# Running sums of the log gates: f32 products replaced by two fp32r passes over split operands

## The chip, the cores and the metric

The kernel runs on one core of one Trainium2 chip. The metric is the device time of one execution in microseconds. The instruction streams of the engines are fixed when the kernel is built; at run time each engine works its own stream off in order and waits at semaphores.

## The reference

One inference step of a hybrid decoder layer, for a prompt of 1024 rows and for 64 sample rows (8 sequences of 8 tokens) with a paged cache. One input projection feeds two groups of heads: gated linear attention (4 heads, dk 64, dv 128) and latent attention (8 heads). Their outputs go through one output projection, a gated MLP with a short convolution, and a gated per-layer embedding. The change touches the linear attention of the prompt:

```python
z = (ga @ lw['gla_w_a2'] + lw['gla_b_a']).astype(jnp.float32)
log_a = (jax.nn.log_sigmoid(z) / GLA_GATE_NORM).reshape(B, T, GLA_HEADS, GLA_DK)   # GLA_GATE_NORM = 16
...
b = jnp.cumsum(log_a, axis=2)              # running sum inside a chunk of tokens
q_dec = q * jnp.exp(b)
k_inv = k * jnp.exp(-b)
k_end = k * jnp.exp(b_last - b)
A = jnp.where(causal, einsum('bnthd,bnshd->bnhts', q_dec, k_inv), 0.0)
...
S = jnp.exp(bl)[..., None] * S + jnp.einsum('bshd,bshv->bhdv', ke, vv)
```

## The kernel before, in words

**Two streams.** The main loop (lines 1598 to 1614) draws from two generators. `dense()` does the prompt: projections of rows 0 to 511 (`prompt_half(0)`), then of rows 512 to 1023 (`prompt_half(1)`), then the linear attention (`gla_prompt`, between its steps also `gla_sample`), then the softmax attention. `cache_stream()` does the attention of the sample rows over the paged cache, in 64 blocks. A block loads `craw` by an indirect DMA on POOL's queue, transposes it on PE (`ctp`, line 522), multiplies it with the weights in `mv` (`ks`, lines 139 to 141, 8 tiles x 2 halves x 3 products), squares and copies the results on ACT (`csq`, `sn`), reduces them on DVE (`css`), adds the rope scores (`csr`), takes the maximum (`mt`), the exponential (`phl`), and multiplies with the values (`cpv`, line 645). POOL works on `sn`, `chl` and `phl`. The generators are interleaved by weights that each dense step yields and by a table `PACE`.

**Who sets the order.** The kernel is written in a tile framework. Tiles come from pools; a tag in a pool names a ring of a few buffers, and a new tile of that tag gets a buffer when an older one has been read for the last time. A scheduler puts the recorded instructions in order for each engine, by their place in the program and by what is ready in its own model of time; so an instruction may stand ahead of others that were written before it. `tc.keep_in_program_order(...)` takes that freedom from an instruction: it stays behind those that were written ahead of it on its engine.

**The second half of the projections.** `prompt_half(1)` transposes its rows (line 798), then computes the latent columns (`ps_lt`, line 278: 4 row tiles x 8 x 3 products of 432 columns). Their weights are loaded through three staging buffers (line 266) and split into a high and a low part (lines 267 to 271). The high parts and half of the low parts lie in three buffers of the ring "w" of the pool `wp`; the other low parts lie in two tiles `wlt` (line 812) of the ring "xin" of the pool `wk`, which has two buffers. The two buffers have held rows of the prompt before (line 769). All further weights of that half (`ps_pj`, `ps_q`, `ps_gv`) come through the same staging buffers and the ring "w".

**The masks.** `gla_weights()` (line 974) is called between the two halves. It builds two masks on POOL, `mq` (128 x 2 x 128) and `mk` (128 x 448), with entries 1/16, 0 and, in `mk`, -1/16; both have buffers of their own in the pool `cp`. The two memsets (lines 982, 983) are kept in program order.

**The step of a tile.** `pre(t)` in `gla_prompt` (line 1138) loads the gate input, `qk` and `gv` of 128 tokens; `log_gate` (line 1004) computes the log gates `la` with a product (`ps_z`, line 1006), three ACT instructions and one of DVE (`z`, line 1012). The running sums are products of `la` with the masks, in f32: four of 128 columns into `ps_b` (line 1149) and two of 448 columns into `ps_bk` (line 1164). ACT takes the exponentials (`qe`, `kx`), DVE scales `q` into `qb` and `qtb` (lines 1156, 1159), POOL scales `k` inside `kx` (line 1168). `local(t)` and `advance(t)` use these for scores, state and output. There are 8 tiles; tile n+2 is in `pre` while n+1 is in `local` and n in `advance`.

`split(hi, lo, src)` (line 115) is used all over the kernel for fp32r operands: ACT copies `src` to `hi` in fp32r, and DVE (or POOL) subtracts, `lo = src - hi`. A product of two split operands is then three single-pass products (`mm3`, line 138).

## Time and profile before

| | |
|---|---|
| times of three runs | 2251.01, 2253.16, 2255.33 us |
| median | 2253.16 us |
| span of the profiled execution, first to last instruction | 2250.3 us |
| mean granted TensorE clock | 0.980 |
| `ps_b` L1149: instructions recorded, median | 64, 275 ns |
| `ps_bk` L1164: instructions recorded, median | 32, 539 ns |
| DMA | 233.60 MB, mean 104 GB/s |

The profiled execution is given by its span; the runs' times include what lies around the span. PE is TensorE (PEld its weight loads), DVE is VectorE, ACT ScalarE, POOL GpSimd, SP the engine that issues most DMAs. L1149 is line 1149 of the kernel. The duration of a matmul in the trace includes its way through the array, so consecutive ones overlap: what a matmul costs in a row of others is the distance from start to start. A row of a timeline or of the chain gives the start, the length and the instruction; a row of a stretch gives its bounds, its length, the busy time and count of PE, PEld, DVE, ACT and POOL, the granted clock, the share of the DMA engines and GB/s; a row of the list of groups gives line, engine, operation, tiles and shapes, count, busy time, mean ns of one, and the idle time ahead of it with what ended it.

### The profile page before, as it was taken

The page shows a single profiled execution, that of the slowest core. Times are in us where ns is not written, and L with a number is a line of the kernel's source. Part 1 is how long each engine was busy: PE and PEld are TensorE (multiplying, and loading weights), DVE is VectorE, ACT ScalarE, POOL GpSimd, SP SyncE. Part 2 cuts the span into 40 slices and gives each one's busy share as a digit, 9 for nine tenths or more (in the row PEclk, how much of TensorE's full clock was granted, in tenths as well). Part 3 has the DMA queues.
Part 4 walks back from the last instruction along what each step waited for, and adds up shares of the span by engine and source line. Part 5 has one row for each costly group of instructions (what it writes and reads, how often), then busy time and mean ns, then how long its engine had stood idle before and what let it go on. Part 6 is the DMA issues. An engine that isn't in the chain of part 4 may idle for free.

```text
span 2250.3 us, 38434 instructions
## 1 busy us (share of the span) xinstructions
PE 2147.8 (95%) x13459; PEld 1937.9 (86%) x13459; DVE 1681.4 (75%) x2490; ACT 1357.9 (60%) x3692; POOL 1356.9 (60%) x1395
## 2 busy tenths in 40 slices
PE   7999989999999999998999988999999999998999
PEld 6889978878888888887888867999999997786899
DVE  4675776467788888886978888888888877966632
ACT  5666766777778898886777775433333334334521
POOL 5675677577777777676455467656566643589000
PEclk9899999999999999999999998999999999999999
DMA  5343244413242222213322222322222228456321
GB/s 184 115 134 102 84 126 147 139 55 88 83 122 59 60 66 74 66 41 100 122 66 78 63 104 62 113 94 90 94 94 96 93 70 291 154 193 206 112 76 37
DMA packets 204547, 233.60 MB, mean 104 GB/s; under 512 B 42430, under 2 KB 146339, under 8 KB 204355
## 3 DMA queue, kind: packets, MB, share of 16 engines
q1 hardware_dynamic: 190691, 184.21, 26.1%
q0 software_dynamic: 12432, 42.48, 6.2%
q10 hardware_dynamic: 1232, 4.46, 0.5%
q8 instruction: 108, 1.77, 0.3%
q14 instruction: 84, 0.69, 0.1%
HBM read 188.52 MB, written 42.52 MB: 103 GB/s over the span
## 4 chain that ended last, share of the span: by engine, by line
PE 71%; DVE 9%; POOL 6%; DMA 5%; ACT 5%; issue 3%; SPq 0%; POOLq 0%; ACTq 0%; DVEq 0%
PE ps_gu L140 7%; PE ps_gu L141 7%; PE ps_gu L139 7%; PE ks L139 4%; PE ks L141 4%; PE ks L140 4%; PE cpv L645 2%; PE ctp L522 2%; DMA raw<-ffn_w_down 2%; PE ps_lt L278 2%; PE ps_pj L139 2%; DVE css L565 1%; PE ps_pj L140 1%; PE ps_pj L141 1%; PE ps_pg L140 1%
## 5 line engine op out<-in xcount | busy, mean ns | idle before, releaser
L560 ACT ACTIVATE csq<-ks 128x256 f32<-128x256 f32 x1040 | 392.4, 400 | 85.6 <-PE ks L141 76.6
L565 DVE TENSOR_REDUCE css<-csq 128x16 f32<-128x1024 f32 (+1 forms) x264 | 315.7, 1197 | 62.9 <-ACT csq L560 59.8
L116 ACT CAST wh<-st 128x512 fp32r<-128x512 f32 x176 | 108.3, 619 | 183.3 <-PE ps_gu L140 163.8
L139 PE MATMUL ks<-mv1h,cTh 128*128 128x320 f32 (+1 forms) x520 | 169.5, 328 | 8.4 <-ACT sn L562 3.6
L139 PE MATMUL ks<-mv0h,cTh 128*128 128x320 f32 (+1 forms) x520 | 170.8, 330 | 6.9 <-ACT csq L560 3.0
L604 POOL TENSOR_TENSOR chl<-craw,chl 128x1024 fp32r<-128x1024 f32 x64 | 141.2, 2206 | 57.3 <-ACT chl L603 56.7
L140 PE MATMUL ks<-mv1l,cTh 128*128 128x320 f32 (+1 forms) x520 | 153.3, 297 | 0.0
L140 PE MATMUL ks<-mv0l,cTh 128*128 128x320 f32 (+1 forms) x520 | 152.1, 294 | 0.0
L141 PE MATMUL ks<-mv0h,cTl 128*128 128x320 f32 (+1 forms) x520 | 147.8, 297 | 0.9 <-DVE cTl L117 0.8
L630 POOL TENSOR_TENSOR phl<-sn,phl 128x512 fp32r<-128x512 f32 (+1 forms) x64 | 84.8, 1326 | 105.0 <-ACT phl L629 104.6
L141 PE MATMUL ks<-mv1h,cTl 128*128 128x320 f32 (+1 forms) x520 | 147.9, 298 | 0.0
L117 DVE TENSOR_TENSOR wl<-st,wh 128x512 fp32r<-128x512 f32 x132 | 119.0, 903 | 29.0 <-ACT wh L116 29.0
L140 PE MATMUL ps_dn<-o 128*128 128x512 f32 x308 | 125.6, 408 | 12.1 <-DVE o L117 12.0
L117 POOL TENSOR_TENSOR wl<-st,wh 128x512 fp32r<-128x512 f32 x44 | 69.1, 1574 | 104.3 <-ACT wh L116 104.3
L139 PE MATMUL ps_dn<-o 128*128 128x512 f32 x308 | 119.6, 399 | 4.5 <-ACT o L116 4.5
L141 PE MATMUL ps_dn<-o 128*128 128x512 f32 x308 | 123.8, 402 | 0.0
L117 DVE TENSOR_TENSOR cTl<-ctp,cTh 128x512 fp32r<-128x512 f32 (+1 forms) x136 | 90.0, 662 | 37.3 <-ACT cTh L116 36.3
L1317 POOL TENSOR_TENSOR pl<-p,ph 128x512 fp32r<-128x512 f32 (+1 forms) x96 | 97.4, 1019 | 33.0 <-DVE ph L1316 23.2
L562 ACT COPY sn<-ks 128x64 f32<-128x64 f32 x520 | 117.1, 225 | 0.0
L139 PEld LDWEIGHTS ks<-mv1h,cTh 128*128 128x128 f32 x520 | 98.8, 190 | 20.7 <-ACT sn L562 7.4
L139 PEld LDWEIGHTS ks<-mv0h,cTh 128*128 128x128 f32 x520 | 97.9, 188 | 20.8 <-ACT sn L562 7.0
L139 PE MATMUL ps_gu<-xrh,wh 128*128 128x320 f32 x352 | 108.6, 309 | 0.9 <-ACT xrh L116 0.9
(675 smaller groups left out, 8019.0 us busy)
## 6 DMA issues: line engine op xcount, KB each, us to landing
raw<-ds SPq DMA_DIRECT2D x77, 256.0 KB
raw<-ffn_w_down SPq DMA_DIRECT2D x66, 256.0 KB
stage<-w_in SPq DMA_DIRECT2D x48, 256.0 KB
st<-ffn_w_gate SPq DMA_DIRECT2D x44, 256.0 KB
st<-ffn_w_up SPq DMA_DIRECT2D x44, 256.0 KB
wr<-ffn_w_down SPq DMA_DIRECT2D x44, 256.0 KB
ds<-cv SPq DMA_DIRECT2D x21, 512.0 KB
oraw<-doT SPq DMA_DIRECT2D x16, 256.0 KB
```

The lines of the kernel that those rows point to most:

```text
L116: act.copy(hi, src)
L117: (lo_eng or dve).tensor_tensor(lo, src, hi.bitcast(F32), ALU.subtract)
L139: pe.matmul(ps, ah, bh, start=first, stop=False)
L140: pe.matmul(ps, ah, bl, start=False, stop=False)
L141: return pe.matmul(ps, al, bh, start=False, stop=last)
L278: pe.matmul(ps, x, w, start=first, stop=last)
L560: act.activation(sq[:, f * 256:f * 256 + 256], ks[:, 0:256], AF.Square)
L562: act.copy(o.sn[:, g0 + i, :], ks[:, 256:320])
L565: dve.tensor_reduce(o.ss[:, g0 + i + 1 - n:g0 + i + 1, :].rearrange("p i h -> p (i h)"), sq2[:, :n].rearrange("p i (h n) -> p (i h) n", n= ...
L604: pool.tensor_tensor(ch[:, c0:c1, 128:256], src, ch[:, c0:c1, 0:128].bitcast(F32), ALU.subtract)
L630: pool.tensor_tensor(phl[:, :nt, 64:128], sb, phl[:, :nt, 0:64].bitcast(F32), ALU.subtract)
L1317: pool.tensor_tensor(pl[:, c0:], p[:, c0:], ph[:, c0:].bitcast(F32), ALU.subtract)
```

## The change

The masks get fp32r buffers of their own (`mqr`, `mkr`). They are built, by the same instructions, in a tile of the ring "xin", and POOL copies them. In the step of a tile the log gates are split in a high and a low half, and each running sum is accumulated over two fp32r products, one for each half. The two parts of `mq` go into one product of 256 columns; for that the axes of `ps_b` and `qe` change places. The reads of `qe` follow.

```diff
@@ -977,8 +977,9 @@
 
         gout = ctile([P, 1], F32, "gout")
         sp.dma_start(gout, A["gla_g_out"].rearrange("o d -> d o"))
-        mq = cst([P, 2, P], F32, "mq")
-        mk = cst([P, 448], F32, "mk")
+        mqr, mkr = cst([P, 2, P], F32R, "mqr"), cst([P, 448], F32R, "mkr")
+        mq = wk.tile([P, D], F32, tag="xin", name="masks")
+        mq, mk = mq[:, 0:256].rearrange("p (i t) -> p i t", i=2), mq[:, 256:704]
         tc.keep_in_program_order(pool.memset(mq, 1.0 / 16))
         tc.keep_in_program_order(pool.memset(mk, 1.0 / 16))
         pool.affine_select(mq, mq, pattern=[[0, 2], [1, P]], compare_op=ALU.is_ge, fill=0.0, base=0, channel_multiplier=-1)
@@ -993,7 +994,9 @@
                                    channel_multiplier=-1)
             if i < 4:
                 pool.tensor_scalar(mk[:, OFFS[i] + 32 * i:OFFS[i + 1]], m4[:, i], -1.0, None, ALU.mult)
-        return gout, mq, mk
+        pool.tensor_copy(mqr, mq)
+        pool.tensor_copy(mkr, mk)
+        return gout, mqr, mkr
 
     def low_rank(g, c0, rows):
 
@@ -1143,30 +1146,36 @@
             gv = g.tile([P, 512], F32, tag="gv", name="gv", bufs=3)
             sp.dma_start(gv, dgv[tt, :])
             la = log_gate(g, gaT, P, wa2)
+            hl = [g.tile([P, 256], F32R, tag="la" + k, name="la" + k) for k in "hl"]
+            split(*hl, la)
+
+            def summed(ps, pr, m):
+                for i, x in enumerate(hl):
+                    pe.matmul(ps, x[:, pr * P:(pr + 1) * P], m, start=i == 0, stop=i == 1)
+
             ps = pd([P, 2, 2, P], "ps_b")
-            for i in range(2):
-                for pr in range(2):
-                    pe.matmul(ps[:, i, pr], la[:, pr * P:(pr + 1) * P], mq[:, i], start=True, stop=True)
+            for pr in range(2):
+                summed(ps[:, pr].rearrange("p i t -> p (i t)"), pr, mq.rearrange("p i t -> p (i t)"))
             qe = g.tile([P, 2, 2, P], F32, tag="qe", name="qe", bufs=3)
             act.activation(qe, ps, AF.Exp)
 
             qbt = qb[t % 2]
             for e in range(2):
                 rr = slice(64 * e, 64 * e + 64)
-                dve.scalar_tensor_tensor(qbt[rr].rearrange("p a i e t -> p (a i) e t")[:, :, e, :],
-                                         qk[rr, 0:2].rearrange("p a (i t) -> p (a i) t", t=32), 0.125,
-                                         qe[rr, 0].rearrange("p a (i t) -> p (a i) t", t=32), ALU.mult, ALU.mult)
-                dve.scalar_tensor_tensor(qtb[t % 3][rr, e::2, :], qk[rr, 0:2], 0.125, qe[rr, 1], ALU.mult, ALU.mult)
+                dve.scalar_tensor_tensor(qbt[rr, :, :, e, :],
+                                         qk[rr, 0:2].rearrange("p a (i t) -> p a i t", t=32), 0.125,
+                                         qe[rr, :, 0].rearrange("p a (i t) -> p a i t", t=32), ALU.mult, ALU.mult)
+                dve.scalar_tensor_tensor(qtb[t % 3][rr, e::2, :], qk[rr, 0:2], 0.125, qe[rr, :, 1], ALU.mult, ALU.mult)
 
             kx = g.tile([P, 2, 448], F32, tag="kx", name="kx")
             for pr in range(2):
                 ps = pd([P, 512], "ps_bk")
-                pe.matmul(ps[:, 0:448], la[:, pr * P:(pr + 1) * P], mk, start=True, stop=True)
+                summed(ps[:, 0:448], pr, mk)
                 act.activation(kx[:, pr], ps[:, 0:448], AF.Exp)
             for i in range(5):
                 w = min(32 * (i + 1), P)
                 pool.tensor_tensor(kx[:, :, offs[i]:offs[i] + w], kx[:, :, offs[i]:offs[i] + w], qk[:, 2:4, 0:w], ALU.mult)
-            dec = [qe[:, 1, pr, P - 1:P] for pr in range(2)]
+            dec = [qe[:, pr, 1, P - 1:P] for pr in range(2)]
             return gv, qbt, kx, dec
 
         def local(t, qbt, kx):
```

## The prediction

> **What bounds the kernel now.** I read the page first, then busy time by stretches, then the chain of waits through the stage that the edit touches.
>
> ```profile
> span 2250.3 us, 38434 instructions
> ...
> PE 2147.8 (95%) x13459; PEld 1937.9 (86%) x13459; DVE 1681.4 (75%) x2490; ACT 1357.9 (60%) x3692; POOL 1356.9 (60%) x1395
> ...
> PEclk9899999999999999999999998999999999999999
> ...
> PE 71%; DVE 9%; POOL 6%; DMA 5%; ACT 5%; issue 3%; SPq 0%; POOLq 0%; ACTq 0%; DVEq 0%
> ```
>
> PE is busy 95% of the span and carries 71% of the chain, so the time is PE's work plus the idle time of PE: 2250.3 = 2147.8 + 102.5. A change counts if it changes either of these. The two stretches below (share of each engine, then granted clock) are the second half of the projections, and the linear-attention stage, which the trace shows from 437.5 us (first ps_z) to 617 us.
>
> ```profile
> 268.00:437.00 169.00, 156.36 (x973) 140.00 (x971) 104.93 (x179) 115.22 (x339) 113.60 (x126) 0.96 0.44 130
> 440.00:620.00 180.00, 175.61 (x1276) 147.73 (x1274) 133.07 (x235) 134.70 (x440) 127.94 (x190) 1.00 0.28 78
> ```
>
> In the linear-attention stage PE has 4.4 us of idle time in 180, DVE and ACT sit at 74 and 75%. All that time the cache stream runs in between: its blocks fill PE wherever the dense stream waits.
>
> **The change part by part. 1: the running sums.** Before, a tile does four f32 products of 128 columns (ps_b) and two of 448 (ps_bk), each recorded as two instructions, so x8 and x4. In the chain (start, length, what) they stand for four of the eight tiles; first and last of the four:
>
> ```profile
> 455.80 0.89 PE ps_b L1149 x8
> 456.69 1.50 PE ps_bk L1164 x4
> ...
> 613.86 0.89 PE ps_b L1149 x8
> 614.75 1.51 PE ps_bk L1164 x4
> ```
>
> That is 2.39 us a tile. After, a tile does four products of 256 columns and four of 448, in fp32r and single pass. Prices of that form: in the timeline three ks products of 256 columns start between 440.68 and 441.03, and the chain has 13 ps_lt products of 432 columns in a row.
>
> ```profile
> 440.68 0.28 PE L139 MATMUL ks<-mv1h,cTh 128*128 128x256 f32 x1
> ...
> 441.03 0.31 PE L139 MATMUL ks<-mv1h,cTh 128*128 128x320 f32 x1
> ...
> 240.58 2.55 PE ps_lt L278 x13
> ```
>
> 256 columns cost 0.35/3 = 0.117 us; 432 cost 2.55/13 = 0.196, so 448 some 0.203. The new tile costs 4 x 0.117 + 4 x 0.203 = 1.28 us, 1.11 less. Over 8 tiles PE loses 8.9 us of work.
>
> **2: the split.** Each tile gains a cast of 128x256 on ACT and a subtraction of 128x256 on DVE, both between z and the first product. Nearest rows:
>
> ```profile
> L116 ACT CAST kTh<-crp 128x256 fp32r<-128x256 f32 x64 | 24.7, 386 | 8.5 <-PE crp L500 7.5 <-DVE css L565 0.3
> L117 DVE TENSOR_TENSOR kTl<-crp,kTh 128x256 fp32r<-128x256 f32 x64 | 26.6, 416 | 20.0 <-ACT kTh L116 19.8
> L117 DVE TENSOR_TENSOR wl<-st,wh 128x512 fp32r<-128x512 f32 x132 | 119.0, 903 | 29.0 <-ACT wh L116 29.0
> ```
>
> ACT 0.39 us. DVE between 0.42 (one operand in PSUM) and 903/2 = 0.45 (both in SBUF, as here): 0.45. So 3.1 us more ACT and 3.6 us more DVE over the stage, both with 45 us of room; what counts is 0.84 us of delay per tile. The products of the low half stand behind cache products in PE's order, so the cache stream covers it where it has work ready. Where the chain runs on ACT or DVE it is paid.
>
> Sum for the stage: the four tiles on the chain gain 1.11 each for certain; of the other four I take half. 6 x 1.11 = 6.7, less the delay for two tiles, 1.7: **-5 us**. Ends: -8.9 (all gained, all delay covered) and -4 x 1.11 + 4 x 0.84 = -1.
>
> The regrouped access of qe and qb leaves counts and elements of the DVE and ACT instructions as they are: nothing. The masks are made by the same POOL instructions and two copies, below.
>
> **3: where the masks are built.** This is the part that the diff hides. mq and mk had a buffer of their own; now they are built in a buffer of the ring "xin" (two buffers), and copied to fp32r. The next users of that ring are the two low halves of the latent weights (wlt, line 812) of the second half of the prompt. The memsets of the masks are kept in program order, so on POOL they come after the work of the cache blocks written ahead of them. Before, that held nobody up: the instruction order on POOL has the first wlt split 46 rows ahead of the memset of mq. In the compiled order of the changed kernel both wlt splits come behind it:
>
> ```
> POOL row 195  L630 phl (cache block)
> POOL row 196  L983 Memset masks
> POOL row 198  L271 wlt (first buffer)
> POOL row 214  L997 mqr<-masks;  row 216  L998 mkr<-masks
> POOL row 219  L271 wlt (second buffer)
> ```
>
> PE follows. Before, the 96 ps_lt products of this half are mixed with 72 cache instructions. After, three ps_lt come early, then none until 192 cache instructions are through (counted from the ks products just ahead of the first ps_lt), then the rest, most of it in one piece. Weights that follow (wp, stage) wait too, because the ps_lt hold their buffers. So for 192 PE instructions, a bit over 2.6 blocks (a block has some 74: 48 ks, 8 cpv, 8 ctp, 2 crp, 6 csr, 2 mt), PE has the cache stream alone. What does that cost? The nearest row is the ten us ahead of the linear-attention stage, where all but two products are the cache's; the best row is five us in which cache and transposes alternate, the worst the second half of the nearest one:
>
> ```profile
> 430.00:440.00 10.00, 7.73 (x56) 7.09 (x57) 5.63 (x7) 7.21 (x26) 10.00 (x15) 1.00 1.11 252
> 230.00:235.00 5.00, 5.00 (x44) 4.99 (x43) 5.00 (x9) 4.87 (x16) 4.66 (x5) 1.00 0.31 91
> 435.00:440.00 5.00, 2.73 (x19) 2.19 (x18) 1.71 (x3) 3.00 (x13) 5.00 (x6) 1.00 1.16 273
> ```
>
> Nearest: 2.27 us idle per 56, so 192/56 x 2.27 = 7.8 us. Best: 0. Worst: 192/19 x 2.27 = 23 us, though POOL is full there with memsets of the next stage. A check by ACT, which must square and copy what PE makes:
>
> ```profile
> L560 ACT ACTIVATE csq<-ks 128x256 f32<-128x256 f32 x1040 | 392.4, 400 | 85.6 <-PE ks L141 76.6 <-DVE css L565 2.9 <-PE csr L141 0.3
> L562 ACT COPY sn<-ks 128x64 f32<-128x64 f32 x520 | 117.1, 225 | 0.0
> L116 ACT CAST cTh<-ctp 128x512 fp32r<-128x512 f32 x128 | 76.0, 594 | 36.2 <-PE ctp L522 35.9
> L603 ACT CAST chl<-craw 128x1024 fp32r<-128x1024 f32 x64 | 67.7, 1057 | 27.9 <-PE cpv L645 11.4 <-issue 8.1 <-POOL sn L594 3.8
> L510 ACT COPY sr<-csr 128x512 f32<-128x512 f32 x64 | 38.7, 604 | 16.5 <-PE csr L141 12.7 <-POOL sn L594 1.6 <-POOL rs_r L112 1.0
> L628 ACT ACTIVATE sn<-sn 128x512 f32<-128x512 f32 x56 | 35.7, 638 | 10.5 <-DVE sn L626 10.5
> L629 ACT CAST phl<-sn 128x512 fp32r<-128x512 f32 x56 | 35.4, 632 | 0.8
> ```
>
> With kTh's 24.7 they make 787.7 us over 64 blocks, 12.3 a block; 2.6 blocks need 32 us of ACT and 192 x 7.73/56 = 26.5 us of PE: 5.5 us idle at least, since ACT would have to run without a gap. I take the nearest row: **+8 us**.
>
> PE's work isn't lost: the cache stream is 112 instructions (1.5 blocks) ahead when the linear attention starts, 108 ahead when the attention starts, level at its end. It comes back as shorter stages. The idle time doesn't: the stages in which it comes back leave PE little idle time (4.4 in 180).
>
> Then the second wlt buffer waits for the mask chain. Before, that chain took, with other POOL work between, from the first to the last of these rows; a copy of 256 columns is the third:
>
> ```profile
> 307.10 0.31 POOL L982 MEMSET mq<- 128x256 f32 x1
> 318.33 1.31 POOL L995 TENSOR_SCALAR mk<-mq 128x32 f32<-128x32 f32 x4
> 293.12 0.46 POOL L944 COPY kt<-lat 128x256 f32<-128x256 f32 x1
> ```
>
> 12.5 us, and 0.46 + 0.80 for the copies: 13.8. PE has, between the first and the second wlt buffer, 54 cache instructions and 18 ps_lt: 54 x 0.138 + 18 x 0.196 = 11.0 us (0.138 is 7.73/56). **+3 us** of waiting, with the ks, csr and cpv of the next block queued behind it on PE; ends 0 (POOL does the chain without a break) and 6 (the cache waits for ACT meanwhile). SP's order loses nothing more: its loads of these weights stand where they stood, and wait for the same buffers.
>
> **Sum:** 2250.3 - 5 + 8 + 3 = 2256.3 us for the profiled execution. The median of the three times shown, 2253.16, lies 2.9 above its span; **2259 us**.
>
> **A rule against the change.** When PE idles the profile shows this, at the hole that the weights' loads leave at 280 us:
>
> ```profile
> 280.00:285.00 5.00, 1.92 (x10) 1.25 (x10) 3.42 (x9) 1.58 (x5) 0.93 (x1) 0.83 0.77 235
> 285.00:290.00 5.00, 3.89 (x11) 3.06 (x12) 2.65 (x4) 3.83 (x12) 2.55 (x2) 0.50 0.68 195
> 350.00:355.00 5.00, 3.02 (x10) 2.80 (x11) 4.95 (x12) 2.68 (x8) 3.53 (x6) 0.65 0.84 233
> 355.00:360.00 5.00, 5.00 (x29) 4.81 (x29) 1.38 (x6) 1.92 (x6) 2.68 (x2) 0.66 1.08 318
> ```
>
> One such hole costs 5 x 0.17 + 5 x 0.50 = 3.4 us of clock beside its idle time, the other 5 x 0.35 + 5 x 0.34 = 3.5. But at 435 us PE was busy 2.73 of 5 at a clock of 1.00: short gaps do not trip it. The Trainium skill, "TensorE: Matmul & The Clock Gate", Part 1: The HAM clock gate, says that an idle window of about 3.4 us halves the clock until a busy window has passed. The trace agrees (0.50 after a hole of 3 us), and by that rule a gap in the cache-only stretch would count only if it is that long.
>
> **The rivals.** A, the forecast, 0.50.
>
> B, the stretch trips the clock: the wait for the masks comes in one piece with nothing of the cache ready. Two holes at 3.5 us on top of the forecast: 2266; or the worst row. For it: PE waits in order, one late ps_lt stops the cache behind it. Against it: the clock of 1.00 at 435 us. 0.14.
>
> C, it comes out even: the cache keeps PE as busy as ACT allows (5.5), the masks are ready in time (0), the stage gains 6: 2253. For it: ACT has 32% of room in the second half. 0.20.
>
> D, faster: the wait takes the place of waits that are there anyway. The trace of before loses 12.6 us of PE between 268 and 437, much of it waiting for weights (the hole at 280 us). If the loads arrive while the cache runs alone, the holes of 275 to 290 us (0.46 + 3.08 + 1.11 = 4.7 and 3.4 of clock) go, and with the 8.9 of the stage against 8 + 3 the time is 2253.2 - 8.9 + 11 - 8.1 = 2247. It decides from the point at which holes of 6 us vanish. Against it: the low halves that wait hold the three staging buffers, so the loads cannot run ahead. 0.16.
>
> That single pass fp32r isn't cheaper I leave out: ks and ps_lt show its price hundreds of times.
>
> **How the numbers follow.** Some 0.2%, 4.5 us, is what a measurement of this kernel can tell from none. A runs from +1 to +12: three quarters of it (0.38) slower, 0.12 within 0.2%. B is slower, C the same, D faster. Slower 0.52, same 0.32, faster 0.16. The range runs from 2246 (D, within a microsecond) to 2272 (stretch near its worst row, or B with a long wait).
>
> **What would show it.** Right: L1154 at some 0.12 and 0.20 us; between 240 and 290 us a stretch with PE at 75 to 85%, ps_lt in two parts around it, and the first ps_z 20 to 30 us later than at 437.5 (112 x 0.138 = 15, and 11 of idle); this lead shrinking to some 6 us by the end of attention. Wrong: PE at 95% or more in that stretch, holes gone at 280 us, or a new hole in the linear-attention stage where PE waits for the split.

## The result, and the profile after

| | median of the runs | runs, lowest to highest |
|---|---|---|
| before | 2252.09 us | 4, 2248.33 to 2255.33 |
| after | 2285.09 us | 4, 2273.94 to 2288.14 |

The ratio is 1.0138, with a 95% interval of 1.0118 to 1.0158. The forecast was 2259, its range 2246 to 2272: the sign was right, the size was not. From the page of the changed kernel, its span, the engines and the shares of the chain:

```profile
span 2284.5 us, 38396 instructions
...
PE 2150.9 (94%) x13427; PEld 1940.8 (85%) x13427; DVE 1691.8 (74%) x2498; ACT 1357.4 (59%) x3700; POOL 1362.4 (60%) x1397
...
PE 50%; DVE 9%; ACT 5%; POOL 4%; issue 3%; DMA 3%; SPq 0%; POOLq 0%; DVEq 0%; ACTq 0%
```

PE's idle time went from 102.5 to 2284.5 - 2150.9 = 133.6 us, and PE's busy time did not fall by the 8.9 us of the forecast, it rose by 3.1. Where this happened is seen when both spans are cut at the same three marks: the first `ps_z`, the first product of the softmax attention, and the first product after it (`pt_cv`). Four stretches of before:

```profile
0.00:437.50 437.50, 402.34 (x2511) 363.87 (x2511) 275.62 (x501) 293.49 (x883) 282.13 (x347) 0.96 0.42 127
437.50:649.40 211.90, 206.93 (x1506) 175.57 (x1507) 158.10 (x276) 158.98 (x523) 149.96 (x212) 1.00 0.30 84
649.40:1144.70 495.30, 476.04 (x3189) 416.24 (x3188) 409.00 (x655) 415.01 (x1237) 345.26 (x346) 0.99 0.27 78
1144.70:2250.30 1105.60, 1062.52 (x6256) 982.19 (x6256) 838.71 (x1060) 490.43 (x1052) 579.53 (x493) 0.98 0.34 110
```

And of after:

```profile
0.00:456.20 456.20, 420.25 (x2625) 379.87 (x2625) 289.16 (x525) 309.90 (x939) 299.81 (x373) 0.98 0.40 124
456.20:679.30 223.10, 204.84 (x1470) 179.25 (x1471) 165.50 (x282) 159.87 (x531) 148.49 (x202) 0.95 0.28 81
679.30:1174.50 495.20, 468.28 (x3079) 404.37 (x3077) 391.25 (x632) 398.20 (x1181) 333.21 (x333) 0.98 0.26 76
1174.50:2284.50 1110.00, 1057.57 (x6256) 977.29 (x6256) 845.92 (x1060) 489.46 (x1052) 580.85 (x493) 0.99 0.33 109
```

Stretches can be compared only for the same work, so the cache stream's progress must be taken out. By the compiled order the changed kernel's cache stream is 112 PE instructions ahead at the first mark, 108 at the second, level at the third (the records in the traces count 114, 110 and 0). At the forecast's 0.138 us for one (an estimate):

| stretch | length | of it cache stream | net | forecast, net |
|---|---|---|---|---|
| to the first `ps_z` | +18.7 | +15.5 | +3.2 | +11 |
| linear attention, L | +11.2 | -0.6 | +11.8 | -5 |
| softmax attention, A | -0.1 | -14.9 | +14.8 | 0 |
| the rest | +4.4 | 0 | +4.4 | 0 |

In L, PE's idle time went from 4.97 to 18.26 us, and the granted clock from 1.00 to 0.95, which is 204.84 x 0.05 = 10.2 us of busy time more. PE's work at full clock fell from 206.9 to 204.84 x 0.95 = 194.6. So the saving was there, 12.3 us with the cache's 0.6; but 13.3 us more of idle time and 10.2 lost to the clock stand against it. What PE waited for in L, after and then before (us in all, times, longest):

```profile
PE csr L141 <- DVE kTl L117: 6.5, 3, 3.0
PE ks L141 <- DVE cTl L117: 4.0, 5, 1.9
PE ks L139 <- ACT cTh L116: 2.6, 5, 0.7
```

```profile
PE ps_z L1006 <- DMA gaT<-dga: 2.3, 1, 2.3
PE ks L139 <- ACT sn L562: 0.8, 3, 0.3
PE mt L625 <- DVE mt L622: 0.8, 1, 0.8
PE ks L141 <- DVE cTl L117: 0.8, 1, 0.8
```

The new waits are those of the cache stream's products for DVE: 6.5 + 4.0 us, where before had 0.8. The timeline of after shows how one comes about (start, length, instruction, idle time ahead of it):

```profile
463.73 0.28 PE L1154 MATMUL ps_b<-mqr,lah 128*128 128x256 f32 x1
...
463.85 0.28 PE L1154 MATMUL ps_b<-mqr,lal 128*128 128x256 f32 x1
...
463.97 0.57 PE L1154 MATMUL ps_bk<-mkr,lal 128*128 128x448 f32 x2
...
465.24 2.17 POOL L604 TENSOR_TENSOR chl<-craw,chl 128x1024 fp32r<-128x1024 f32 x1
...
465.49 2.20 DVE L1165 SCALAR_TENSOR_TENSOR qb<-qk,qe 64x256 f32<-64x256 f32 x1
...
467.37 3.39 POOL L1177 TENSOR_TENSOR kx<-kx,qk 128x64 f32<-128x64 f32 x5
467.62 0.53 DVE L1168 SCALAR_TENSOR_TENSOR qtb<-qk,qe 64x256 f32<-64x256 f32 x1
468.16 0.58 DVE L1165 SCALAR_TENSOR_TENSOR qb<-qk,qe 64x256 f32<-64x256 f32 x1
468.67 0.81 DVE L1168 SCALAR_TENSOR_TENSOR qtb<-qk,qe 64x256 f32<-64x256 f32 x1
469.51 0.29 DVE L117 TENSOR_TENSOR kTl<-crp,kTh 128x128 fp32r<-128x128 f32 x1
```

```profile
469.86 0.30 PE L141 MATMUL csr<-qbd0h,kTl 128*128 128x64 f32 x1 [2.91 <-DVE kTl L117]
```

The `qb` product on DVE lasts 2.20 us (median of 16: 0.438); it began just after POOL's 2.17 us product and ended just after it. Three more follow, all a little long beside POOL's next products, then the cache's small `kTl`, for which PE has stood 2.91 us. Five us apiece around it, PE's busy time first, the clock third from the end:

```profile
465.00:470.00 5.00, 1.73 (x11) 1.39 (x11) 4.95 (x8) 2.16 (x7) 4.96 (x6) 1.00 0.01 3
470.00:475.00 5.00, 5.00 (x28) 4.33 (x29) 1.83 (x5) 1.80 (x6) 3.92 (x5) 0.55 0.57 162
475.00:480.00 5.00, 5.00 (x26) 4.24 (x26) 0.52 (x3) 4.06 (x17) 2.02 (x2) 0.77 0.07 26
```

DVE is busy 4.95 of 5 us in the hole. The hole costs 3.27 us of idle time, and 2.25 + 1.15 = 3.4 us of clock behind it.

### The profile page after: what moved, and what is told of

Read it like the earlier page. It is cut to its first block, busy times and chain, and to the rows that moved or that the text cites. A ratio compares the mean times of both kernels' runs of the same rounds, so it can differ in the third digit from the quotient of the medians.

```text
span 2284.5 us, 38396 instructions
## 1 busy us (share of the span) xinstructions
PE 2150.9 (94%) x13427; PEld 1940.8 (85%) x13427; DVE 1691.8 (74%) x2498; ACT 1357.4 (59%) x3700; POOL 1362.4 (60%) x1397
## 4 chain that ended last, share of the span: by engine, by line
PE 50%; DVE 9%; ACT 5%; POOL 4%; issue 3%; DMA 3%; SPq 0%; POOLq 0%; DVEq 0%; ACTq 0%
PE ps_gu L141 7%; PE ps_gu L139 7%; PE ps_gu L140 7%; PE ks L139 3%; PE ks L141 2%; PE ks L140 2%; DVE o L117 2%; PE ps_pg L140 1%; PE ps_pg L141 1%; PE ps_pg L139 1%; PE cpv L645 1%; ACT csq L560 1%; DMA raw<-ffn_w_down 1%; PE ctp L522 1%; PE ps_dn L140 1%
## 5 line engine op out<-in xcount | busy, mean ns | idle before, releaser
L140 PE MATMUL ps_dn<-o 128*128 128x512 f32 x308 | 124.0, 402 | 16.2 <-DVE o L117 16.2
L139 PE MATMUL ps_dn<-o 128*128 128x512 f32 x308 | 118.4, 393 | 4.5 <-ACT o L116 4.5
L141 PE MATMUL ps_dn<-o 128*128 128x512 f32 x308 | 121.6, 395 | 0.0
L141 PE MATMUL ps_gu<-xrh,wl 128*128 128x320 f32 x352 | 108.7, 309 | 0.0
```

Source lines behind the costliest of these rows:

```text
L139: pe.matmul(ps, ah, bh, start=first, stop=False)
L140: pe.matmul(ps, ah, bl, start=False, stop=False)
L141: return pe.matmul(ps, al, bh, start=False, stop=last)
```

## The experiments

All eighteen runs in one table. L and A are the lengths of the two stretches, brought to the cache progress of the kernel before (871 and 2063 instructions, at 0.138 us for each that a kernel has more or fewer; an estimate). DVE is its busy time in L, brought to 871 in the same way at 0.098 us, the difference of 158.10 and 152.80 us between before and e9, divided by their 54 instructions. "Ahead" is the cache stream's lead over before at the start of A. Before measured 2250.8 to 2253.1 beside them. The times are medians of several executions, L, DVE and A those of the one that was profiled. Executions of one kernel lie up to 14 us apart (the changed kernel: 2273.94 to 2288.14), and the profiled one can lie at the edge: that of e12 is the fastest of its ten, that of e13 the slowest of its four. So a difference of two or three us in L or A between two rows says little by itself.

| kernel | median | ratio, 95% interval | L | DVE | ahead | A |
|---|---|---|---|---|---|---|
| before | 2252.1 | | 211.9 | 158.1 | 0 | 495.3 |
| after | 2285.1 | 1.0118 to 1.0158 | 223.7 | 165.9 | 108 | 510.1 |
| e1 masks in place | 2258.0 | 1.0016 to 1.0036 | 220.0 | 170.3 | -6 | 493.4 |
| e2 ring only | 2271.3 | 1.0066 to 1.0100 | 212.8 | 157.7 | 84 | 506.5 |
| e3 no pin | 2258.5 | 1.0018 to 1.0046 | 220.5 | 163.3 | 9 | 498.4 |
| e4 split unused | 2269.5 | 1.0062 to 1.0095 | 215.8 | 162.5 | -54 | 506.0 |
| e5 e1, kx on DVE | 2267.8 | 1.0063 to 1.0101 | 225.6 | 177.5 | -62 | 494.8 |
| e6 before, kx on DVE | 2255.3 | 1.0007 to 1.0027 | 223.3 | 165.3 | -69 | 485.6 |
| e7 high half | 2261.6 | 1.0028 to 1.0069 | 210.1 | 160.8 | -54 | 502.7 |
| e8 low on POOL | 2286.3 | 1.0144 to 1.0178 | 225.5 | 166.7 | 84 | 510.3 |
| e9 before, one column | 2264.6 | 1.0039 to 1.0082 | 212.6 | 158.1 | -54 | 503.3 |
| e10 before, DVE copy | 2254.8 | 1.0001 to 1.0029 | 214.8 | 162.9 | 0 | 496.6 |
| e11 merge in f32 | 2264.8 | 1.0038 to 1.0081 | 212.7 | 158.7 | -54 | 504.4 |
| e12 direct | 2259.8 | 1.0020 to 1.0046 | 213.9 | 159.5 | -62 | 496.9 |
| e13 direct, filled | 2273.8 | 1.0075 to 1.0112 | 216.5 | 161.0 | -3 | 505.6 |
| e14 high twice | 2266.8 | 1.0048 to 1.0082 | 220.6 | 171.2 | 9 | 501.2 |
| e15 high by DVE | 2289.6 | 1.0146 to 1.0182 | 226.9 | 170.9 | -60 | 515.0 |
| e16 after, one column | 2273.2 | 1.0079 to 1.0113 | 218.9 | 162.7 | 167 | 505.8 |
| e17 e1, column on ACT | 2276.7 | 1.0064 to 1.0115 | 220.6 | 171.3 | -17 | 506.3 |
| e18 e1, column on DVE | 2274.2 | 1.0074 to 1.0116 | 218.4 | 169.5 | -22 | 503.1 |

**First theories.** The ring theory: the masks' buffer with the pinned memsets makes the whole loss. The split theory: the split's two steps, in the queues of ACT and DVE, make it.

### e1: masks built in their own fp32r buffers

```diff
-        mq = wk.tile([P, D], F32, tag="xin", name="masks")
-        mq, mk = mq[:, 0:256].rearrange(...), mq[:, 256:704]
+        mq, mk = mqr, mkr
...
-        pool.tensor_copy(mqr, mq)
-        pool.tensor_copy(mkr, mk)
```

> The changed kernel, but the masks are built in their fp32r buffers themselves, without the tile of the ring xin and without the two copies; the order of the instructions ahead of the linear attention is then that of the kernel before. Ring theory (the place of the masks makes the second half of the projections late, and all of the 34 us of span follow from that): 2242 to 2252 us, the first ps_z at 437 us as before, and the linear attention 5 us shorter than before. Split theory (the split itself makes the linear attention longer, by the 12 us that it lost there): 2260 to 2270 us, with holes of PE in the linear attention and a clock under 1.00 there.

### e2: the kernel before, masks built in the ring and copied to f32 buffers

```diff
+        mqr, mkr = cst([P, 2, P], F32, "mqr"), cst([P, 448], F32, "mkr")
+        mq = wk.tile([P, D], F32, tag="xin", name="masks")
...
+        pool.tensor_copy(mqr, mq)
+        pool.tensor_copy(mkr, mk)
```

> The kernel before, with its f32 sums, but the masks are built in a tile of the ring xin and copied by POOL to f32 buffers; no split. Ring theory: 2275 to 2295 us, as the changed kernel, with the last ps_lt of the second half at 304 us in place of 269. Split theory: 2255 to 2265 us, since the first ps_z came only 3 us late beyond the cache instructions that were done ahead, and nothing more is lost in the linear attention.

### e3: the changed kernel, memsets not kept in program order

```diff
-        tc.keep_in_program_order(pool.memset(mq, 1.0 / 16))
+        pool.memset(mq, 1.0 / 16)
```

(the same for `mk`)

> The changed kernel, but the two memsets of the masks are not kept in program order; the masks still pass through the ring xin. In the order of the instructions ps_lt then stands where it stood before. Ring theory with the pin as its cause: 2242 to 2255 us. If it is the ring alone (a buffer less for the latent weights): 2275 us or more. Split theory: 2260 to 2270 us.

### e4: the kernel before, with the split made and not used

```diff
             la = log_gate(g, gaT, P, wa2)
+            hl = [g.tile([P, 256], F32R, tag="la" + k, name="la" + k) for k in "hl"]
+            split(*hl, la)
```

> The kernel before with the split of the log gates added (cast on ACT, subtraction on DVE) but not used: the sums are the f32 products of la as before. Prices the split by itself. Ring theory: 2250 to 2258 us (0.84 us a tile, mostly beside other work). Split theory: 2260 us or more.

e1 and e3 took 27 us off the changed kernel and came out between the two answers; e2, the ring by itself, cost 18, less than the ring theory asked and more than the split theory. e4 fitted the split theory's number, but not its place: L rose by 3.9 us, A by 10.7, where no split runs. So neither theory stood, and something acted far from the edits. The expectations that follow count a stage's loss as idle time and clock together, and their linear-attention stage ends at the last `ps_z`; the table's L goes on to the attention.

### e5: e1 with the multiplication of kx on DVE

```diff
-                pool.tensor_tensor(kx[:, :, offs[i]:offs[i] + w], ...
+                dve.tensor_tensor(kx[:, :, offs[i]:offs[i] + w], ...
```

> The masks are built in place and summed in fp32r as in the run with masks in place, and the five multiplications of kx per tile, which POOL does there, go to DVE. I count the loss of a stage as its length less PE's busy time weighted with the granted clock; in the linear-attention stage it is 4.3 us before the change and 20.7 with the masks in place. Theory of the shared operand reads (DVE's products of qk and qe are stretched while POOL multiplies kx): one of the two partners is gone, the 32 products qb and qtb take 13 to 15 us in all instead of 25.4, the loss of the stage falls to 4 to 11. Rival, the split's delay (two more steps on ACT and DVE ahead of the sums, with PE's later work queued behind): DVE gets about 1.3 us more a tile in the same queue, the loss of the stage stays at 18 to 28. The attention stage, which starts in this order 62 cache instructions of PE behind the kernel before, loses 23 to 27 us if only the order of the linear attention matters, 33 to 37 if any shift of the cache stream's position at its start costs as it seemed to in the run with the unused split. Time by the first theory 2242 to 2250 with the attention undisturbed and some 10 more if not; by the rival 2256 to 2268.

### e6: the kernel before with the same edit

> The kernel before, with f32 sums, and the five multiplications of kx per tile on DVE instead of POOL. Both theories of the linear-attention stage expect its loss at 3 to 8 us (4.3 before): there is no split, and the products of qk and qe are hardly stretched before the change. It is the yardstick for the run with kx on DVE and the masks in place, and a test of the attention stage by itself: the order has the cache stream 69 PE instructions behind the kernel before at its start. If such a shift costs, the attention stage loses 33 to 37 us instead of 25.4, and the time is 2258 to 2266; if it does not, 2250 to 2256.

### e7: e1, high half alone

```diff
-            split(*hl, la)
+            act.copy(hl[0], la)
```

> The masks in place, and the sums over the high half of the log gates alone: the low half, its subtraction on DVE and its second pass on PE are left out. PE loses about 0.64 us a tile of work more, 5 us in all. Theory of the split's delay: the loss of the linear-attention stage falls from 20.7 to 4 to 10 us, since the subtraction and what waits for it are gone; time 2238 to 2248 plus what the attention stage loses. Theory of the shared operand reads: POOL multiplies kx as before, all the sums still arrive together, so qb and qtb stay stretched (20 to 26 us for 32) and the loss stays at 13 to 22; time 2248 to 2258. The order has the cache stream 54 PE instructions behind at the start of the attention: if that costs, about 10 us more in that stage in either case.

### e8: e1, subtraction on POOL

```diff
-            split(*hl, la)
+            split(*hl, la, pool)
```

> The masks in place, and the subtraction of the low half on POOL instead of DVE. POOL takes about 0.7 us for it where DVE takes 0.45. Theory of the split's delay through DVE's queue: DVE is free of it, the loss of the linear-attention stage falls to 8 to 15 us. Theory of the shared operand reads: POOL gets one more instruction with two operands, qb and qtb stay stretched, the loss stays at 17 to 25. The order has the cache stream 84 PE instructions ahead of the kernel before at the start of the attention, about as far as in the kernels with the masks in the ring; if a shift costs in that stage, it loses 32 to 38 us there instead of 23 to 26, and the time is 2262 to 2270; if not, 2250 to 2260.

The shared reads as the only cause fell: in e5 `kx`, one partner of the products of `qk` and `qe`, has left POOL, and L is 5.6 us longer than in e1; the loss of the stage, 26.6, is the rival's. But the 32 products still took 19.9 us, not 13 to 15, beside POOL's other products, so e5 took the partners away only in part. e6 missed both answers in L, 11.4 us longer for the 40 small products that DVE took over, and has the shortest A of all, so a cache stream behind does not cost as such. In e7 (the low half left out) the loss was 16, as the shared reads had it, but the 32 products took 18.3 us, not 20 to 26. Without the subtraction and the second pass L is 210.1, ten less than e1, though ACT still casts; and its 14 us of saved work on PE made L only 1.8 shorter than before. In e8 the loss of 23.5 is the shared reads' too; its time is above both answers, with A at 510.3. POOL needs 0.74 us for each of these subtractions, and PE waits 2.7 us for one of them, so e8 also added a delay of its own.

### e9: the kernel before and a copy of one column on ACT

```diff
             la = log_gate(g, gaT, P, wa2)
+            act.copy(g.tile([P, 1], F32, tag="nul", name="nul"), la[:, 0:1])
```

> The kernel before, and in each tile of the linear attention one copy on ACT of one column of the log gates into a tile that nothing reads. Eight such copies are about 1 to 2 us of ACT, which has room. But the order of the instructions moves with it: the cache stream is 54 PE instructions behind the kernel before at the start of the attention, the same number as in the runs with the unused split and with the high half alone. Theory of the order (what a stage loses depends on which order comes out, and any edit of this code draws another): the attention stage loses 31 to 38 us instead of 25.4, the linear-attention stage 4 to 10 instead of 4.3, time 2256 to 2266. Rival, the work (what was added costs, the order does not): attention 24 to 27, linear attention 4 to 6, time 2250 to 2254.

The eight copies have a median of 0.238 us. The two stretches L and A of this kernel:

```profile
L1146 ACT COPY nul<-z x8: 185/238/319, 443.0 to 614.8; 128x1 f32<-128x1 f32 x8
```

```profile
438.60:643.70 205.10, 198.67 (x1453) 168.72 (x1454) 152.80 (x267) 153.30 (x508) 148.03 (x210) 1.00 0.31 87
643.70:1154.20 510.50, 484.17 (x3241) 422.99 (x3239) 415.62 (x666) 422.31 (x1260) 348.53 (x349) 0.99 0.25 76
```

Two us of ACT cost the whole kernel 14: the theory of the order holds. (Which order the scheduler happens to give an edit is called its draw below.) L is what it was (idle time 6.4 of 205.1, clock 1.00). A has 52 cache instructions more to do (54 at its start, of which 2 are left at its end), 7.2 us, and is 15.2 longer.

### e10: the kernel before and a copy of 256 columns on DVE

```diff
+            dve.tensor_copy(g.tile([P, 256], F32, tag="nul", name="nul"), la[:, 0:256])
```

> The kernel before, and in each tile of the linear attention one copy on DVE of the 256 columns of the log gates into a tile that nothing reads: about 0.3 us of DVE a tile ahead of the products of qk and qe, with two operands in SBUF counted with its output. The cache stream stands in the order where it stood before at each mark that I compared. Theory of the order: time 2249 to 2255, the linear-attention stage loses 4 to 8 us. Theory of the split's work on DVE: 8 times 0.3 of work and more of stretching behind it, the stage loses 8 to 14, time 2255 to 2262.

### e11: the kernel before with the masks merged, in f32

```diff
-            for i in range(2):
-                for pr in range(2):
-                    pe.matmul(ps[:, i, pr], la[...], mq[:, i], start=True, stop=True)
+            for pr in range(2):
+                pe.matmul(ps[:, pr].rearrange(...), la[...], mq.rearrange(...), start=True, stop=True)
```

(and the exchanged axes of `qe`)

> The kernel before, with only the two masks merged: two f32 products of 256 columns for the four of 128, and the axes of qe exchanged. PE's work is the same but for two products less of fixed cost a tile. The order has the cache stream 54 PE instructions behind at the start of the attention. Theory of the order: as the run with one column, attention 31 to 38 us of loss, linear attention 4 to 10, time 2256 to 2266. Rival, the merge itself (the results of all sums come together, the products of qk and qe meet POOL's kx): linear attention 12 to 20 of loss, time 2260 to 2272. If neither acts, 2249 to 2254.

e11 is e9 again: 2264.8, L 212.7, A 504.4. The merge by itself does nothing in L. e10 gave 2254.8 and a loss of 7.7 in the stage, both at the upper edge of the order's answer. Its order keeps its marks, and A is 496.6; L took 2.9 us more. Where the order draws the same number at the start of A, A comes out alike, whatever the edit was: 502.7 to 506.0 for the four kernels at -54, 495.3 and 496.6 for the two at 0. By their traces, before and e10 have the same order of instructions throughout A on PE, DVE, ACT and POOL, and e4 and e9 differ there by the place of one ACT instruction: the same order gave the same A within 1.3 and 2.7 us. The number by itself decides nothing. e13 (below) starts A at -3 and has 505.6; in its trace the cache stream falls up to 75 instructions behind before's in the midst of A.

### e12: DVE writes the log gates in fp32r, one pass

```diff
-        dve.scalar_tensor_tensor(z[:rows], ps[:rows, 0:256], 0.0, e[:rows], ...
+        dve.scalar_tensor_tensor(z[:rows] if out is None else out, ps[:rows, 0:256], 0.0, e[:rows], ...
```

(`out` is the fp32r tile of the one pass; the masks are in place, the low half is left out)

> Masks in place, and DVE writes the log gates in fp32r at once: no cast, no subtraction, one pass in fp32r. The low half is left out. The chain to the sums is then that of the kernel before, and PE has about 14 us of work less over the stage (2.39 to 0.64 us a tile). Theory that PE bounds the stage: 10 to 14 us of it come out as time, loss of the linear-attention stage 4 to 9, time 2238 to 2246, 6 to 10 more if the order hurts the attention. Rival, that ACT and DVE pace the stage and PE's freed time stays idle: loss 14 to 20 in that stage, time 2249 to 2260.

### e13: e12 with three more passes that nothing reads

```diff
+                for _ in range(3):
+                    pe.matmul(ps, hl[0][:, pr * P:(pr + 1) * P], m, start=True, stop=True)
```

> The kernel that has DVE write the log gates in fp32r (low half left out), with each product of the sums issued three more times ahead of the one that counts: nothing reads them. PE gets 3 times 0.64 us a tile back, 15 us over the stage, so it has about the work of the kernel before; ACT and DVE have what they had. Linear attention up to the start of the attention took 205.3 us with 809 cache instructions; this order has 868, 8 us more at 0.138. Theory that ACT and DVE pace the stage: the added work goes into what was idle, stage and way to the attention 211 to 216 us, idle 4 to 7 and clock loss 0 to 2 in the stage. Theory that PE bounds it and only the clock ate the gain: 8 of clock come back, but 15 of work are added, 218 to 224 us with the same idle time of 9 to 12. Time by the first 2250 to 2258, by the second 2258 to 2268.

The stretch L of e12, then of e13:

```profile
438.00:643.30 205.30, 190.43 (x1380) 165.27 (x1381) 153.46 (x264) 150.32 (x494) 146.95 (x210) 0.96 0.30 85
```

```profile
440.70:656.80 216.10, 209.01 (x1536) 182.13 (x1537) 160.70 (x277) 158.54 (x519) 153.05 (x214) 1.00 0.30 85
```

In e12 the chain to the sums is that of before and PE has some 14 us less to do, yet L is 2.0 us longer for the same progress; 14.9 us are idle and 190.43 x 0.04 = 7.6 are clock. In e13 PE gets 15 us back that nobody needs, and L grows by 2.6. Idle time falls to 7.1 and the clock is whole again. The stretch itself, 216.1, lies at the upper edge of the first theory (211 to 216) and below the second (218 to 224): PE does not pace this stage. The time, 2273.8, missed both answers. As a whole e13 is 13.9 us slower than e12; 8.7 us of difference lie in A, where none of the added products runs.

### e14: e1 with one more pass of the high half

```diff
+                pe.matmul(ps, hl[0][:, pr * P:(pr + 1) * P], m, start=True, stop=True)
```

> The kernel with the masks in place and both halves, and one more pass of the high half ahead of the two that count: 0.64 us a tile of PE work that nothing needs, 5 us in all. Linear attention up to the start of the attention took 219.2 us with 865 cache instructions; this order has 880. If PE bounds the stage: 226 us, time 2262 to 2268. If ACT and DVE pace it: 219 to 222, and the idle time falls by 5 with the clock loss at most what it was, time 2254 to 2260.

L for the same progress: 220.6 against 220.0 in e1, for 5 us more on PE. That is the answer of ACT and DVE; the time is the other answer's, for A lost 5.9 against before.

### e15: no cast; DVE writes high half, gate and difference

```diff
+            dve.scalar_tensor_tensor(hl[0], ps[:, 0:256], 0.0, e, ALU.min, ALU.subtract)
+            dve.scalar_tensor_tensor(z, ps[:, 0:256], 0.0, e, ALU.min, ALU.subtract)
+            dve.tensor_tensor(hl[1], z, hl[0].bitcast(F32), ALU.subtract)
```

> Masks in place and both halves, but no cast on ACT: DVE writes the high half straight from the gate's last step in fp32r, then the gate in f32, then the difference. The high half's products can start when they could before the change; DVE has one more instruction of 128x256 a tile than with the cast, ACT one less. If the delay of the cast is what the split costs: the stage's loss falls from 20.7 to 10 to 16 us, time 2248 to 2256 (this order has the cache stream 60 behind at the start of the attention, where 0 to 9 us more were lost). If DVE's queue is: 20 to 28, time 2258 to 2268.

L is 6.9 us above e1 for one more DVE instruction a tile and one less on ACT, the answer of DVE's queue. Yet DVE's busy time in L is only 0.6 above e1's, so it isn't the sum of DVE's work that made L longer. The 2289.6 are beyond both answers, as A lost most of all (515.0).

### e16: the changed kernel and a copy of one column on ACT

The edit of e9.

> The changed kernel, and in each tile one copy on ACT of one column of the log gates that nothing reads. The work is the same but for 1 to 2 us of ACT. The order has the cache stream 167 PE instructions ahead of the kernel before at the start of the attention, 59 more than in the changed kernel. If the lead comes back as shorter stages: 2283 to 2289. If a lead is lost for the most part: 59 times 0.138 is 8 us, of which the attention returns little, 2289 to 2297.

The stretches L and A:

```profile
458.70:685.20 226.50, 212.33 (x1531) 186.33 (x1532) 168.07 (x294) 167.79 (x565) 158.16 (x212) 0.96 0.29 83
685.20:1168.00 482.80, 459.71 (x3019) 396.44 (x3018) 385.57 (x620) 391.87 (x1156) 325.91 (x326) 0.98 0.26 77
```

Both answers missed: the kernel with more to do is 12 us faster than the changed one. Its lead is larger, and A is 12.4 us shorter than in the changed kernel, of which 59 x 0.138 = 8.1 is the larger lead.

### e17 and e18: e1 and a copy of one column, on ACT and on DVE

> Masks in place and both halves, and in each tile one copy on ACT of one column of the log gates that nothing reads. The order has the cache stream 17 PE instructions behind the kernel before at the start of the attention (6 without the copy). If the 6 us of the kernel with the masks in place are a price of the split, the linear attention up to the start of the attention stays at 219 to 222 us for 865 cache instructions and only what follows is drawn anew; time 2255 to 2272. If they are a draw, that stretch may come out at 212 or less, and the time below 2252.

> The same with the one-column copy on DVE. The order has the cache stream 22 PE instructions behind the kernel before at the start of the attention. As for the copy on ACT: price of the split 2255 to 2272 with 219 to 223 us for 865 cache instructions between the first ps_z and the attention; a draw if that stretch is 212 or less.

L stays at 220.6 and 218.4: the split's price in L is no draw. The times are 2276.7 and 2274.2 where e1 had 2258.0: A is 493.4 in e1, a good draw, and 506.3 and 503.1 in these two, beside the 505.8 of e16. So the 27 us between the changed kernel and e1 can't be read as the price of the ring: over their draws, the kernels with the ring have 2273 and 2285, those with the masks in place 2258, 2274 and 2277.

## Why the prediction failed, step by step

The forecast took PE's saved work as time in L and priced A and the rest at nothing. L came out 11.8 us longer where 5 less was forecast, A 14.8 longer and the rest 4.4; only the stretch before the masks came out with the sign that was forecast, below its price. The last sign of being wrong that the prediction names came nearly as written: new holes of PE in the linear attention, though PE waits there for the cache's `kTl` and `cTl` behind DVE's other work and not for the split itself.

**The running sums, -8.9 of PE's work.** The work fell as forecast, or somewhat more: the timeline above has `ps_b` products 0.12 us apart, and the work in L fell by 12.3 at full clock, 0.6 of it the cache's (the rounding of the clock alone is 1 us). **This step failed in the sentence "the four tiles on the chain gain 1.11 each for certain".** The chain ran through PE there because PE was always busy, not because the stage waited for it. e12 and e13 show it: 15 us more or less of PE's work move L by 2.6. What does pace L is not settled. Over the 20 kernels L goes with DVE's busy time in it (correlation 0.80), not with PE's work at full clock (-0.3), and e5, e6 and e10, which add to DVE, have a longer L. But that busy time holds DVE's own waits for POOL, and among the seven kernels with the whole split the correlation is gone (-0.05): DVE is busy 163.3 us in e3 and 171.3 in e17, and L is 220.5 and 220.6. So the place of DVE's instructions in its queue, as in the timeline above, may count for more than their sum; neither that nor a part of ACT was tried apart.

**The split, 0.84 us of delay a tile and 45 us of room.** Its DVE work was mis-sized, and room by a share of busy time was the wrong measure. In the list of groups, before and then after:

```profile
L1156 DVE SCALAR_TENSOR_TENSOR qb<-qk,qe 64x256 f32<-64x256 f32 x16 | 8.7, 547 | 3.0 <-ACT qe L1151 2.8
L1159 DVE SCALAR_TENSOR_TENSOR qtb<-qk,qe 64x256 f32<-64x256 f32 x16 | 8.4, 524 | 0.0
```

```profile
L1168 DVE SCALAR_TENSOR_TENSOR qtb<-qk,qe 64x256 f32<-64x256 f32 x16 | 11.2, 702 | 0.0
L1165 DVE SCALAR_TENSOR_TENSOR qb<-qk,qe 64x256 f32<-64x256 f32 x16 | 10.8, 677 | 1.1 <-ACT qe L1160 1.0
L117 DVE TENSOR_TENSOR lal<-z,lah 128x256 fp32r<-128x256 f32 x8 | 3.6, 446 | 0.0
```

The subtraction costs the 3.6 us of the forecast. The products of `qk` and `qe`, whose number and shape I had as unchanged, cost 22.0 instead of 17.1, 4.9 more, since more of them now meet POOL's products: 8 of the 32 last over 0.7 us, where before had 3. (In e1 the three groups take 14.0, 11.4 and 6.3; the regrouping of `qe` alone, in e11, has the two at 19.9.) The seven kernels with both halves and `kx` on POOL, the subtraction on DVE and the cast on ACT have L at 218.4 to 223.7; before, e2, e9 and e11, without the split, at 211.9 to 212.8. So the price of the split and the fp32r sums together is 6 to 12 us in L, where I had -5.

**The stretch before the masks, +11.** The place was right and the price too high. The thirty us with the cache alone, the place of the old hole, and a new one:

```profile
240.00:270.00 30.00, 25.86 (x178) 22.99 (x177) 23.53 (x38) 24.87 (x86) 20.89 (x23) 1.00 0.14 45
```

```profile
280.00:290.00 10.00, 8.39 (x52) 7.43 (x53) 8.64 (x10) 7.50 (x27) 8.74 (x10) 1.00 0.44 131
...
310.00:320.00 10.00, 6.21 (x31) 5.12 (x31) 7.25 (x19) 6.76 (x18) 4.49 (x5) 0.85 0.60 177
320.00:330.00 10.00, 10.00 (x43) 8.95 (x42) 3.76 (x10) 4.44 (x14) 4.10 (x5) 0.81 0.20 54
```

PE was 86% busy, just above the 75 to 85 that I had named, with 4.1 us of idle time for 178 instructions where my row gave 7.2. That row was misread: all of its 2.27 us of idle time is one wait of `ps_z` for the load of `gaT` (shown below), not the cache stream's. In part rival D came true: the hole at 280 us closed to 1.6 us of idle time at a clock of 1.00. But a hole of 3.8 us stands at 310 us instead, with 0.9 + 1.9 us of clock. The net is +3.2, and in all three kernels with ring and pin the first `ps_z` comes at 456.2 to 458.7 us, in all others at 434.2 to 440.7.

**"It comes back as shorter stages."** This failed. The lead of 108 did go, but A stayed as long: 26.92 us of idle time against 19.26, and a clock of 0.98 for 0.99. The row of e16 shows that a lead can shorten A. The four kernels with a lead of 84 or more have A at 505.8 to 510.3, the 15 others besides before at 485.6 to 515.0, 500.9 on average. Against that average such a lead loses some 7 us, which lies within the spread of the others; some 6 of the 14.8 are that before has a good draw. What in an order makes A longer was not tried and stays open. So do the 4.4 us of the rest; over the 20 kernels that last stretch takes 1103.9 to 1115.0 us.

**The rivals.** B, the clock, had 0.14. As written it did not come: from 240 to 270 us the clock is 1.00. The clock was lost in L, 10.2 us, which no rival had. And what the prediction held against B, that short gaps do not trip the clock, does not hold. PE has the same wait ahead of the first `ps_z` in both kernels, before and then after, with the five us around the latter:

```profile
437.48 0.69 PE L1006 MATMUL ps_z<-wa,gaT 17*128 17x256 f32 x2 [2.27 <-DMA gaT<-dga]
```

```profile
456.16 0.69 PE L1009 MATMUL ps_z<-wa,gaT 17*128 17x256 f32 x2 [2.14 <-DMA gaT<-dga]
```

```profile
455.00:460.00 5.00, 3.84 (x15) 3.51 (x16) 1.22 (x1) 2.74 (x10) 4.75 (x8) 0.69 1.10 329
```

Before, the clock stayed at 1.00 behind 2.27 us; after, 2.14 us brought it to 0.69 in these five us, 1.55 us of clock and part of the 10.2. So the length of a wait alone does not decide. The Trainium skill, "TensorE: Matmul & The Clock Gate", Part 1, has a window of about 3.4 us; here waits of 2.14 us and, in the row at 470 us, of 2.91 were enough, and the measurement decides. C, which came out even, and D, which was faster, both needed the saving in L.

**What is shown and what is not.** Shown: PE's saved work is not time in L; the split lengthens L, in seven orders; the changed kernel's lead bought it no shorter A; a change of 2 us of ACT moves the whole by 12 to 19 us either way, and where two kernels have the same order in A, A is the same within 3 us. Not shown: what paces L, what in an order lengthens A, and how much of the 33 us is this draw. With the one-column copy in both kernels the change costs 2273.2 - 2264.6 = 9 us.

## What to carry to other kernels

A stage in which PE is 98% busy need not be paced by PE: ask what PE would wait for if it had less to do, and look at the queues of the engines that feed the stream that fills it. Where a scheduler sets the order, add an instruction that does nothing before an edit is priced, here worth up to 19 us: an effect of that size from one pair of kernels says little about the edit. Do not count a lead of a background stream as time gained before the stage that gets it back has been measured: here 108 instructions ahead made A 0.1 us shorter, 167 ahead 12.5.

## What the runs showed of the hardware

A DVE product of two operands in SBUF that starts while a POOL product runs waits for it: in the timeline 2.20 us for 0.44, ending 0.28 us behind POOL's. Of the 32 such products in L of the changed kernel, the 12 that started with no POOL instruction under way took at most 0.42 us; the 8 of over 0.7 us each ended 0.28 to 0.33 us behind a POOL product. The Trainium skill, "SBUF — State Buffer", SBUF: two separate sides, calls the port pair that the two engines share "an exclusive lock, not a bandwidth split"; the timeline agrees. And PE work that nothing needs cost the stage that it stands in little: in e13 15 us of it made L 2.6 us longer than in e12, while the idle time fell from 14.9 to 7.1 us and the clock rose from 0.96 to 1.00. That is L alone; the kernel as a whole was 13.9 us slower.
